# RWKV low-rank products in plain float32, the key norm by tokens, and HGRN projections on the unscaled operand, in a two-layer hybrid decoder on one core

## The chip, the cores and the metric

The kernel runs on one core of one Trainium2 chip. The metric is device time in microseconds (us) of one execution; lower is better. The core has TensorE (PE in the profile; PEld is its weight load), VectorE (DVE), ScalarE (ACT), GpSimd (POOL) and SyncE (SP), which here only issues the weight transfers. Each engine works through its own instruction list in order and waits where a semaphore is not there yet.

## The reference

Two layers, 256 tokens, width 1024, float32. Each layer normalises the hidden state, multiplies it by one wide matrix `w_in`, and feeds column groups to four mixers (RWKV-7, dilated attention, mLSTM, HGRN2). Their outputs are projected, gated, summed and multiplied by `w_out`; a gated feed-forward network follows. What matters here, cut from the reference:

```python
def rwkv7_branch(z, mu, w0, w2, a0, a2, g2, k_k, ...):
    z = z + mu * (token_shift(z) - z)
    r, k, v, wl, al, gl = split_cols(z, [256, 256, 256, 32, 32, 64])
    logw = -softplus(-(w0 + tanh(wl) @ w2)) - 0.5      # low rank 32
    a = sigmoid(a0 + al @ a2)                          # low rank 32
    g = sigmoid(gl) @ g2                               # low rank 64
    kk = heads(k * k_k)                                # 4 heads of 64
    kk = kk * rsqrt(sum(kk * kk, axis=-1, keepdims=True) + 1e-12)
    ...
def hgrn2_branch(z, lower_bound, norm_g):
    q, f, i, g = split_cols(z, [256] * 4)
    ...
# z = rmsnorm(x, gain) @ w_in ; rmsnorm = x * gain * rsqrt(mean(x*x) + eps)
```

The row factor of the norm, `R = rsqrt(mean(x*x) + eps)`, is one number for each token. It may be applied to the operand ahead of the product, or to the product.

## The kernel before, in words

**Precision by splitting.** Weights arrive in blocks of 128 x 1024 (512 KB) in three buffers `raw`. ACT rounds a block to `hi` (line 301) and DVE forms `lo = raw - hi` (line 302). A product takes three reduced-precision (fp32r) matmuls for each 128 x 128 weight tile: hi by hi, hi by lo, lo by hi (lines 351 to 353), 24 for each 128 output columns. SP fetches a block into a `raw` buffer once the `lo` of an earlier block has freed it. Four pairs of `hi` and `lo` may be ahead of TensorE.

**Operand.** `X["u"]` (tiles `xh`, `xl`) is the hidden state times the gain, without the row factor, split in two. `X["s"]` (tiles `sh`, `sl`) is the same with the row factor: `scaled_block` (line 448) forms `xsc` on DVE (line 454) or on ACT and POOL (lines 451, 452), ACT rounds it to `sh` (line 445) and POOL forms `sl` (line 446), for eight blocks. A product on `X["u"]` needs the factor afterwards.

**Row factor.** Two products with a column of ones (`psrm`, line 424) give the sums of squares by token; DVE scales them (`rcm`, line 426); POOL raises them to the power -1/2 (line 427); two products (`psbm`, line 434) spread the result over the partitions, and ACT copies it to `R` (`Rm`, line 437).

**Start of a layer's mixers.** `rw_cols` makes seven RWKV column blocks on `X["u"]` (PSUM tiles `rw`, three PSUM buffers) and evacuates each with `R` into `zr` (lines 610 and 648); between the evacuations it calls `scale`, which makes `X["s"]`. `hg_cols` makes the HGRN columns: `hgq` on `X["u"]` in both layers, `hgf` on `X["u"]` in layer 0 and on `X["s"]` in layer 1, then `hgt` by tokens on `X["s"]`. The gates (`gate`) and everything behind use `X["s"]`.

**RWKV preparation**, a background generator whose pieces are slipped between the large products. It mixes neighbouring tokens (line 659), splits the low-rank weights `lort` into `lw` and the low-rank inputs into `la` (ACT line 670, DVE line 671), stacks the parts on 96 partitions, and multiplies in fp32r (`psw`, `psa`, lines 699 and 700; `psg`, lines 717 and 718). The key norm sums squares by head with a block matrix `bd` (`pss`, line 726), then takes a logarithm and an exponential on ACT (lines 733 and 734), each with a load of ACT's function table.

**Order.** The instruction order of each engine is fixed when the program is built: a scheduler places instructions by its own estimates of when inputs are ready, with the weight splits at a raised priority.

Of the kernel before, what the change touches and what calls it, by code (L numbers as in the profile page):

```python
# [9 lines left out]
F32 = mybir.dt.float32  # L10
# [211 lines left out]
def trunk(tc, x, wst, prm, rows, lora, fing, cfd, cid, out, dbg=None, depth=DEPTH):  # L222
# [160 lines left out]
    def tok_group(name, cols, mid=None):  # L383

        pss = [pmm.tile([128, 512], F32, name=f"{name}{h}", tag="mm") for h in range(2)]
        for kh in range(4):
            hi, lo = w_next()
            for h in range(2):
                for k in range(2):
                    kk = kh * 2 + k  # L390
                    mm3(pss[h][:, :cols], X["s"][0][:, kk, h * 128:(h + 1) * 128], X["s"][1][:, kk, h * 128:(h + 1) * 128],
                        hi[:, k * cols:(k + 1) * cols], lo[:, k * cols:(k + 1) * cols], kk == 0, kk == 7)
# [99 lines left out]
    for l in range(depth):  # L492
        with ExitStack() as lx:
# [12 lines left out]
            with ExitStack() as mxs:  # L506
# [48 lines left out]
                def project(b, kn, m2, quiet=False):  # L555
# [18 lines left out]
                    if m2 == 0:  # L574
                        mop = mp("mop", bufs=1)
                        pad(mop, "padm", 128)
# [26 lines left out]
                R = None  # L603

                def rw_cols():
                    nonlocal R
# [5 lines left out]
                    def scale(ms):  # L612
                        for m in ms:
                            if m % 2 == 0:
                                tmp = gtp.tile([128, 2, T], F32, name="xsc", tag="gt")
                            scaled_block(m, P("gmix", m) if l else pr0[:, m:m + 1], R, tmp[:, m % 2, :])

                    u = X["u"]
                    ps0 = ct_group("rw0", outer=(l > 0), a=u)
                    rc = None  # L620
# [20 lines left out]
                    scale(range(0, 4))  # L641
                    evac(1, ps1)
                    scale(range(4, 8))
# [6 lines left out]
                def rwkv():  # L650
# [18 lines left out]
                    lw = rw.tile([128, 4, 256], F32R, name="lw", tag="bk")  # L669
                    hi_ = lambda d, s_: ac.copy(d, s_)  # L670
                    lo_ = lambda d, s_, h_: ve.tensor_tensor(d, s_, h_.bitcast(F32), op=OP.subtract)
                    for i, r in ((0, 0), (1, 32)):
                        src = lort[r:r + 32, :]
                        hi_(lw[0:32, i], src)
                        hi_(lw[32:64, i], src)
                        lo_(lw[64:96, i], src, lw[r:r + 32, i])
                    hi_(lw[64:128, 2], lort[64:128, :])
                    hi_(lw[0:64, 2], lort[64:128, :])
                    lo_(lw[64:128, 3], lort[64:128, :], lw[64:128, 2])
                    la = rw.tile([128, 3, T], F32R, name="la", tag="ar")  # L680
                    lr = rw.tile([128, T], F32, name="lr", tag="rtmp", bufs=2)
                    ac.activation(lr[0:32, :], zm[0:32, 6, :], AF.Tanh)
                    hi_(la[0:32, 0], lr[0:32, :])
                    hi_(la[64:96, 0], lr[0:32, :])
                    lo_(la[32:64, 0], lr[0:32, :], la[0:32, 0])
                    za_ = zm[32:64, 6, :]
                    hi_(la[32:64, 1], za_)
                    hi_(la[64:96, 1], za_)
                    lo_(la[0:32, 1], za_, la[32:64, 1])
                    ac.activation(lr[64:128, :], zm[64:128, 6, :], AF.Tanh, scale=0.5)  # L690
                    ve.tensor_scalar(lr[64:128, :], lr[64:128, :], 0.5, 0.5, op0=OP.mult, op1=OP.add)
                    hi_(la[64:128, 2], lr[64:128, :])
                    lo_(la[0:64, 2], lr[64:128, :], la[64:128, 2])
# [15 lines left out]
                    sq = rw.tile([128, 2, T], F32, name="rsq", tag="rtmp", bufs=2)  # L709
# [15 lines left out]
                    pss = PS["rw"].tile([128, 2, T], F32, name="pss", tag="rw")  # L725
                    te.matmul(flat(pss), C("bd"), flat(sq), start=True, stop=True)
# [5 lines left out]
                    nk = rw.tile([128, 2, T], F32, name="nk", tag="rtmp", bufs=2)  # L732
                    ac.activation(nk, pss, AF.Ln, bias=eps12)
                    ac.activation(nk, nk, AF.Exp, scale=-0.5)
# [15 lines left out]
                    for n in range(2):  # L750
                        ve.tensor_tensor(bk[0:64, n, :, 1, :], ch(k2)[0:64, n], ch(Wn)[0:64, n], op=OP.mult)
                        ve.tensor_tensor(bk[64:128, n, :, 0, :], ch(k2)[64:128, n], ch(Wn)[64:128, n], op=OP.mult)
                    kk = kkr
                    ve.tensor_tensor(kk, kkr, nk, op=OP.mult)
# [198 lines left out]
                def hg_cols(zz):  # L953
                    for i, nm in enumerate(("q", "f")):
                        direct = l == 0 or i == 0
                        ps = ct_group("hg" + nm, **({"a": X["u"]} if direct else {}))[0][1]
# [598 lines left out]
```

## Time and profile before

| | us |
|---|---|
| median of three runs | 955.33 |
| lowest and highest run | 949.43, 957.17 |
| the profiled execution's own time | 955.37 |
| its span in the trace | 953.5 |

The span is the stretch from the first to the last recorded instruction; the rest of the execution's time, 1.9 us, lies around it. The profile gives each engine's busy time, the idle time ahead of an instruction with what ended it, and the clock that TensorE was granted (1.00 is 2.4 GHz, 0.50 is 1.2 GHz).

### The profile page before, as it was taken

The page shows a single profiled execution, that of the slowest core. Times are in us where ns is not written, and L with a number is a line of the kernel's source. Part 1 is how long each engine was busy: PE and PEld are TensorE (multiplying, and loading weights), DVE is VectorE, ACT ScalarE, POOL GpSimd, SP SyncE. Part 2 cuts the span into 40 slices and gives each one's busy share as a digit, 9 for nine tenths or more (in the row PEclk, how much of TensorE's full clock was granted, in tenths as well). Part 3 has the DMA queues.
Part 4 walks back from the last instruction along what each step waited for, and adds up shares of the span by engine and source line. Part 5 has one row for each costly group of instructions (what it writes and reads, how often), then busy time and mean ns, then how long its engine had stood idle before and what let it go on. Part 6 is the DMA issues. An engine that isn't in the chain of part 4 may idle for free.

```text
span 953.5 us, 22170 instructions
## 1 busy us (share of the span) xinstructions
PE 928.6 (97%) x9072; PEld 880.2 (92%) x9072; DVE 720.6 (76%) x1136; ACT 569.7 (60%) x968; POOL 226.3 (24%) x226
## 2 busy tenths in 40 slices
PE   8899999999999999999999999999999999999996
PEld 6888999999999999999998899999989999999885
DVE  6898566678688998876678975567768889988643
ACT  7784455665466676664478644555745667866533
POOL 2500141111317621110142004211103474211002
PEclk9999999999999999999999999999999999999998
DMA  7544444345475476556555434444536646656561
GB/s 276 177 135 132 126 149 142 134 154 166 144 216 183 146 221 199 187 174 197 189 172 181 147 98 125 154 155 122 188 123 189 201 138 215 230 189 200 182 193 66
DMA packets 48981, 160.12 MB, mean 168 GB/s; under 512 B 5872, under 2 KB 7408, under 8 KB 48752
## 3 DMA queue, kind: packets, MB, share of 16 engines
q1 hardware_dynamic: 46800, 155.03, 50.9%
q10 hardware_dynamic: 1728, 2.62, 0.9%
q8 instruction: 71, 1.16, 0.5%
q0 software_dynamic: 352, 1.06, 0.4%
q14 instruction: 30, 0.25, 0.1%
HBM read 156.06 MB, written 1.05 MB: 165 GB/s over the span
## 4 chain that ended last, share of the span: by engine, by line
PE 74%; DVE 10%; ACT 5%; POOL 4%; issue 4%; DMA 2%; POOLq 0%; SPq 0%; ACTq 0%; DVEq 0%
PE up L353 6%; PE up L351 6%; PE up L352 6%; PE gate L351 6%; PE gate L353 5%; PE gate L352 5%; PE dn L351 4%; PE dn L353 4%; PE dn L352 4%; DVE lo L302 4%; POOL sl L446 2%; POOL xsc L1432 2%; ACT hi L301 2%; DMA raw<-in_wst_dram 1%; PE at L351 1%
## 5 line engine op out<-in xcount | busy, mean ns | idle before, releaser
L302 DVE TENSOR_TENSOR lo<-raw,hi 128x1024 fp32r<-128x1024 f32 (+4 forms) x316 | 377.8, 1201 | 164.7 <-ACT hi L301 155.7
L301 ACT CAST hi<-raw 128x1024 fp32r<-128x1024 f32 (+4 forms) x316 | 307.4, 978 | 275.2 <-PE up L352 47.8
L353 PE MATMUL up<-sh,lo 128*128 128x256 f32 x544 | 152.2, 280 | 0.8 <-DVE lo L302 0.8
L351 PE MATMUL up<-sh,hi 128*128 128x256 f32 x544 | 152.0, 279 | 0.0
L352 PE MATMUL up<-sl,hi 128*128 128x256 f32 x544 | 151.9, 279 | 0.0
L351 PE MATMUL gate<-sh,hi 128*128 128x256 f32 x512 | 146.5, 286 | 0.0
L353 PE MATMUL gate<-sh,lo 128*128 128x256 f32 x512 | 143.0, 279 | 0.0
L352 PE MATMUL gate<-sl,hi 128*128 128x256 f32 x512 | 142.6, 279 | 0.0
L353 PEld LDWEIGHTS up<-sh,lo 128*128 128x128 f32 x544 | 103.4, 190 | 1.4 <-DVE lo L302 1.4
L352 PEld LDWEIGHTS up<-sl,hi 128*128 128x128 f32 x544 | 102.2, 188 | 0.0
L351 PEld LDWEIGHTS up<-sh,hi 128*128 128x128 f32 x544 | 102.2, 188 | 0.0
L351 PEld LDWEIGHTS gate<-sh,hi 128*128 128x128 f32 x512 | 96.5, 188 | 2.3 <-issue 0.2
L353 PEld LDWEIGHTS gate<-sh,lo 128*128 128x128 f32 x512 | 96.2, 188 | 0.6
L352 PEld LDWEIGHTS gate<-sl,hi 128*128 128x128 f32 x512 | 96.3, 188 | 0.4
L1457 POOL TENSOR_TENSOR af<-sf,cvf 128x256 f32<-128x256 f32 x44 | 45.9, 1043 | 157.8 <-ACT sf L1455 157.8
L1453 DVE SCALAR_TENSOR_TENSOR cvf<-up,pr,cvf 128x255 f32<-128x255 f32 (+1 forms) x136 | 65.1, 479 | 2.4
L572 POOL TENSOR_TENSOR merged<-merged,gt 128x512 f32<-128x512 f32 x16 | 26.6, 1666 | 114.3 <-DVE gt L570 114.3
L352 PE MATMUL dn<-alo,hi 128*128 128x256 f32 x176 | 49.5, 281 | 0.0
L353 PE MATMUL dn<-ahi,lo 128*128 128x256 f32 x176 | 49.5, 281 | 0.0
L351 PE MATMUL dn<-ahi,hi 128*128 128x256 f32 x176 | 49.4, 281 | 0.0
L352 PE MATMUL up<-xl,hi 128*128 128x256 f32 x160 | 44.8, 281 | 0.0
L353 PE MATMUL up<-xh,lo 128*128 128x256 f32 x160 | 44.6, 280 | 0.1
(468 smaller groups left out, 2370.0 us busy)
## 6 DMA issues: line engine op xcount, KB each, us to landing
raw<-in_wst_dram SPq DMA_DIRECT2D x254, 512.0 KB, 3.5
raw<-in_wst_dram SPq DMA_DIRECT2D x16, 448.0 KB, 3.2
raw<-in_wst_dram SPq DMA_DIRECT2D x26, 256.0 KB, 2.8
raw<-in_wst_dram SPq DMA_DIRECT2D x8, 392.0 KB, 3.2
zrot<-zrot ACTq DMA_DIRECT2D x24, 64.0 KB, 3.1
cft<-in_cf_dram SPq DMA_DIRECT2D x1, 1041.0 KB, 7.4
hT<-in_x_dram SPq DMA_DIRECT2D x4, 256.0 KB, 6.0
raw<-in_wst_dram SPq DMA_DIRECT2D x8, 128.0 KB, 2.6
```

The source lines that it names most:

```text
L301: ac.copy(hi[:, c], r[:, c])
L302: ve.tensor_tensor(lo[:, c], r[:, c], hi[:, c].bitcast(F32), op=OP.subtract)
L351: te.matmul(o, lh, rh, start=first, stop=False)
L352: te.matmul(o, lh, rl, start=False, stop=False)
L353: te.matmul(o, ll, rh, start=False, stop=last)
L446: gp.tensor_tensor(lo[:, m, :], tmp, h[:, m, :].bitcast(F32), op=OP.subtract)
L572: gp.tensor_tensor(mo, mo, g, op=OP.add)
L1432: gp.tensor_tensor(xsc[:, m, :], xsc[:, m, :], R, op=OP.mult)
L1453: ve.scalar_tensor_tensor(cv[:, n, d:], z[:, n, 0:T - d], P("fcw", 44 * i + cj), cv[:, n, d:], op0=OP.mult, op1=OP.add)
L1457: gp.tensor_tensor(a_, s, cv[:, 0, :], op=OP.mult)
```

## The change

1. `hgf` in layer 1 and `hgt` in both layers use `X["u"]`. The factor is applied at evacuation: to `hgf` by DVE with `R`, to `hgt` by ACT, as its scale operand with one number for each token (`rc`, and half of it, `rch`, a new small DVE instruction).
2. `scale`, which makes `X["s"]`, stands in the program behind the evacuations of `hgq` and `hgf` instead of between those of `rw_cols`.
3. The low-rank products are plain float32 products from the parameters as they lie; the eleven ACT roundings and six DVE subtractions of a layer go.
4. The key norm is by tokens: four small products with an indicator of two heads (`psn`), a DVE addition, a power on POOL (`rn`), and eight products with the identity that spread the result again (`pnk`), which DVE reads from PSUM. The wide product, the logarithm, the exponential and the two table loads go.

```diff
-    def tok_group(name, cols, mid=None):
+    def tok_group(name, cols, mid=None, a=None):
+        ah, al = a or X["s"]
...
                     evac(0, ps0)
-                    scale(range(0, 4))
                     evac(1, ps1)
-                    scale(range(4, 8))
                     evac(2, ps2 or ct_group("rw2", a=u))
...
-                    lw = rw.tile([128, 4, 256], F32R, name="lw", tag="bk")
...
-                        hi_(lw[0:32, i], src)
-                        hi_(lw[32:64, i], src)
-                        lo_(lw[64:96, i], src, lw[r:r + 32, i])
...
-                        te.matmul(psw[:, n, :], lw[0:96, 0, n * 128:(n + 1) * 128], la[0:96, 0], start=True, stop=True)
-                        te.matmul(psa[:, n, :], lw[0:96, 1, n * 128:(n + 1) * 128], la[0:96, 1], start=True, stop=True)
+                        te.matmul(psw[:, n, :], lort[0:32, n * 128:(n + 1) * 128], lr[0:32, :], start=True, stop=True)
+                        te.matmul(psa[:, n, :], lort[32:64, n * 128:(n + 1) * 128], zm[32:64, 6, :], start=True, stop=True)
...
-                        te.matmul(psg[:, h, :], la[:, 2, h * 128:(h + 1) * 128], lw[:, 2], start=True, stop=False)
-                        te.matmul(psg[:, h, :], la[64:128, 2, h * 128:(h + 1) * 128], lw[64:128, 3], start=False, stop=True)
+                        te.matmul(psg[:, h, :], lr[64:128, h * 128:(h + 1) * 128], lort[64:128, :], start=True, stop=True)
...
-                    te.matmul(flat(pss), C("bd"), flat(sq), start=True, stop=True)
+                    psn = PS["rw"].tile([128, 2, 2, 2], F32, name="psn", tag="rw")
+                    for h in range(2):
+                        for n in range(2):
+                            te.matmul(psn[:, h, n, :], sq[:, n, h * 128:(h + 1) * 128], C("ind"), start=True, stop=True)
+                    rn = rw.tile([128, 2, 8], F32, name="rn")
+                    ve.tensor_scalar(rn[:, 0, :], psn.rearrange("p h n q -> p (h n q)"), 1e-12, None, op0=OP.add)
+                    gp.tensor_tensor(rn[:, 1, :], rn[:, 0, :], nhalf, op=OP.pow)
...
-                    ac.activation(nk, pss, AF.Ln, bias=eps12)
-                    ac.activation(nk, nk, AF.Exp, scale=-0.5)
...
+                                te.matmul(pnk[q * 64:q * 64 + 64, n, h * 128:(h + 1) * 128], rn[:, 1, i:i + 1].to_broadcast([128, 64]),
+                                          ident, start=True, stop=True)
-                    ve.tensor_tensor(kk, kkr, nk, op=OP.mult)
+                    ve.tensor_tensor(kk, kkr, pnk, op=OP.mult)
...
-                        if direct:
-                            ve.tensor_tensor(z, ps, bc2(R, 2), op=OP.mult)
-                        else:
-                            ac.copy(z, ps)
+                        ve.tensor_tensor(z, ps, bc2(R, 2), op=OP.mult)
                         zz[nm] = z
-                    pss = tok_group("hgt", 512)
+                        scale(range(i * 4, i * 4 + 4))
+                    pss = tok_group("hgt", 512, a=X["u"])
+                    rch = zp.tile([128, 2], F32, name="rch")
+                    ve.tensor_scalar(rch, rc[:, 0:2], 0.5, None, op0=OP.mult)
...
-                        ac.activation(V[:, h, :], pss[h][:, 0:256], AF.Copy)
-                        ac.activation(tg[:, h, :], pss[h][:, 256:512], AF.Tanh, scale=0.5)
+                        ac.activation(V[:, h, :], pss[h][:, 0:256], AF.Copy, scale=rc[:, h:h + 1])
+                        ac.activation(tg[:, h, :], pss[h][:, 256:512], AF.Tanh, scale=rch[:, h:h + 1])
```

The order that the scheduler makes differs at three places of which the prediction speaks. First TensorE in layer 0, third RWKV column group (`rw_351`; a number behind a name is a buffer). Before, `psbm`, which spreads the row factor, stood 26 products behind `psrm`; here are its nearest neighbours:

```order
L424 MATMUL psrm_345<-ones,acc 128x1 x2
L351 MATMUL rw_351<-xh,hi_232 128x256
L352 MATMUL rw_351<-xl,hi_232 128x256
L353 MATMUL rw_351<-xh,lo_233 128x256
...
L352 MATMUL rw_351<-xl,hi_265 128x256
L434 MATMUL psbm_383<-ident_t,rcm_348 128x128 x2
L353 MATMUL rw_351<-xh,lo_266 128x256
```

Now:

```order
L425 MATMUL psrm_345<-ones,acc 128x1 x2
L351 MATMUL rw_351<-xh,hi_232 128x256
L352 MATMUL rw_351<-xl,hi_232 128x256
L435 MATMUL psbm_383<-ident_t,rcm_348 128x128 x2
L353 MATMUL rw_351<-xh,lo_233 128x256
```

`psbm` moved forward by 24 products and stands two behind `psrm`.

Second, DVE at the same place: the splits `lo`, the row factor `rcm`, and the evacuations `zr`. Before (numbers of the blocks kept):

```order
L302 TENSOR_TENSOR lo4_233<-raw4_193,hi4_232 128x1024
L426 TENSOR_SCALAR rcm0_348<-psrm0_345 128x2
L302 TENSOR_TENSOR lo5_266<-raw5_195,hi5_265 128x1024
L302 TENSOR_TENSOR lo6_318<-raw6_230,hi6_317 128x1024
L302 TENSOR_TENSOR lo7_356<-raw7_263,hi7_355 128x1024
L302 TENSOR_TENSOR lo8_391<-raw8_315,hi8_390 128x1024
L610 TENSOR_TENSOR zr_185<-rw0_187,Rm0_386 128x2x256
```

Now:

```order
L427 TENSOR_SCALAR rcm0_348<-psrm0_345 128x2
L302 TENSOR_TENSOR lo4_233<-raw4_193,hi4_232 128x1024
L949 TENSOR_SCALAR rch_819<-rcm0_348 128x2
L302 TENSOR_TENSOR lo5_266<-raw5_195,hi5_265 128x1024
L617 TENSOR_TENSOR zr_185<-rw0_187,Rm0_386 128x2x256
L617 TENSOR_TENSOR zr_185<-rw1_260,Rm0_386 128x2x256
L455 SCALAR_TENSOR_TENSOR xsc_567<-hT_73,pr0_71,Rm0_386 128x256
...
L455 SCALAR_TENSOR_TENSOR xsc_688<-hT_73,pr0_71,Rm0_386 128x256
L302 TENSOR_TENSOR lo6_318<-raw6_230,hi6_317 128x1024
```

Two evacuations and four `xsc` now stand ahead of the split of block 6; before, the splits of blocks 6 to 8 stood ahead of the first evacuation. `rch` reads the power's result.

Third, ACT at the same place. Before, the copy of the row factor stood behind the roundings of blocks 4 to 8; the last of these and the copy:

```order
L301 CAST hi7_355<-raw7_263 128x1024
L301 CAST hi8_390<-raw8_315 128x1024
L437 COPY Rm0_386<-psbm0_383 128x256
```

Now:

```order
L301 CAST hi5_265<-raw5_195 128x1024
L438 COPY Rm0_386<-psbm0_383 128x256
L301 CAST hi6_317<-raw6_230 128x1024
```

The copy stands ahead of the rounding of block 6. In layer 1 these three places keep their order but for `rch`, which stands one split behind `rcm`. In both layers `psn` stands right ahead of `hgt` and `pnk` 31 products of `hgt` behind it. From about the middle of the gates of HGRN on, TensorE's order is the same in both programs.

## Rows read from the trace of the kernel before

**Rows 1.** The page: busy time and share of each engine.

```profile
PE 928.6 (97%) x9072; PEld 880.2 (92%) x9072; DVE 720.6 (76%) x1136; ACT 569.7 (60%) x968; POOL 226.3 (24%) x226
```

**Rows 2.** TensorE's waits by releaser, 20 to 90 and 480 to 560 us: total, times, longest.

```profile
PE rw L351 <- DVE zr L610: 2.7, 1, 2.7
PE pv L773 <- ACT Vt L781: 0.7, 1, 0.7
PE psrm L424 <- DVE acc L418: 0.6, 1, 0.6
PE psw L699 <- DVE la L671: 0.5, 1, 0.5
...
PE rw L351 <- DVE zr L610: 1.3, 1, 1.3
PE pv L773 <- ACT Vt L781: 1.1, 1, 1.1
```

**Rows 3.** Two windows: length, busy of PE, PEld, DVE, ACT, POOL, granted clock, DMA.

```profile
30.00:40.00 10.00, 7.80 (x54) 7.80 (x55) 9.68 (x12) 8.23 (x20) 9.36 (x10) 0.83 0.40 127
490.00:500.00 10.00, 8.65 (x76) 8.48 (x75) 9.31 (x12) 8.12 (x17) 7.77 (x9) 1.00 0.47 159
```

**Rows 4.** Timeline of PE, layer 0: start, length, instruction, idle time before it.

```profile
22.21 0.61 PE L424 MATMUL psrm<-ones,acc 128*128 128x1 f32 x4 [0.58 <-DVE acc L418]
...
32.20 0.40 PE L351 MATMUL rw<-xh,hi 128*128 128x256 f32 x1 [2.65 <-DVE zr L610]
...
36.66 0.28 PE L351 MATMUL hgq<-xh,hi 128*128 128x256 f32 x1
36.78 0.28 PE L352 MATMUL hgq<-xl,hi 128*128 128x256 f32 x1
```

**Rows 5.** Timelines of ACT and POOL, layer 0.

```profile
27.44 1.05 ACT L301 CAST hi<-raw 128x1024 fp32r<-128x1024 f32 x1 [3.37 <-DMA raw<-in_wst_dram]
30.19 0.37 ACT L437 COPY Rm<-psbm 128x256 f32<-128x256 f32 x1
...
23.59 1.62 POOL L427 TENSOR_TENSOR rcm<-rcm,nhalf 128x2 f32<-128x2 f32 x1 [2.42 <-DVE rcm L426]
```

**Rows 6.** Timeline of DVE, layer 0.

```profile
23.42 2.35 DVE L302 TENSOR_TENSOR lo<-raw,hi 128x1024 fp32r<-128x1024 f32 x2
31.46 0.69 DVE L610 TENSOR_TENSOR zr<-rw,Rm 128x512 f32<-128x512 f32 x1
32.06 1.93 DVE L454 SCALAR_TENSOR_TENSOR xsc<-hT,pr,Rm 128x256 f32<-128x256 f32 x2
```

**Rows 7.** Timeline of ACT, layer 1.

```profile
487.10 2.52 ACT L670 CAST lw<-lort 32x256 fp32r<-32x256 f32 x6 [1.61 <-DMA lort<-in_lora_dram]
...
492.50 0.36 ACT L437 COPY Rm<-psbm 128x256 f32<-128x256 f32 x1
```

**Rows 8.** Timeline of PE, layer 0, low-rank gate product and sums of squares.

```profile
53.84 0.28 PE L717 MATMUL psg<-lw,la 128*128 128x256 f32 x1
54.98 1.13 PE L726 MATMUL pss<-rsq,cft 128*128 128x512 f32 x2
55.54 0.80 PE L352 MATMUL hgt<-lo,sh 128*128 128x512 f32 x1
56.18 0.40 PE L353 MATMUL hgt<-hi,sl 128*128 128x512 f32 x1
```

**Rows 9.** Timelines of PE: plain float32 products elsewhere (a product leaves two records).

```profile
228.40 1.57 PE L1309 MATMUL pS<-cv 64*128 64x256 f32 x12
...
77.01 1.16 PE L792 MATMUL pl<-ar,bk 64*128 64x128 f32 x8
...
89.59 0.95 PE L807 MATMUL psq<-cft,prod 128*128 128x2 f32 x8
```

**Rows 10.** Timelines of ACT (squares of the key, layer 0) and POOL (a power of eight columns).

```profile
48.83 0.63 ACT L712 ACTIVATE rsq<-w4b 128x512 f32<-128x512 f32 x1
...
115.10 1.66 POOL L1131 TENSOR_TENSOR hst<-hst,nhalf 128x8 f32<-128x8 f32 x1 [14.23 <-DMA zrot<-zrot]
```

More of the change, by code (lines that the diff above doesn't have):

```diff
@@ L390, in tok_group @@
                     kk = kh * 2 + k
-                    mm3(pss[h][:, :cols], X["s"][0][:, kk, h * 128:(h + 1) * 128], X["s"][1][:, kk, h * 128:(h + 1) * 128],
+                    mm3(pss[h][:, :cols], ah[:, kk, h * 128:(h + 1) * 128], al[:, kk, h * 128:(h + 1) * 128],
                         hi[:, k * cols:(k + 1) * cols], lo[:, k * cols:(k + 1) * cols], kk == 0, kk == 7)
@@ L575, in project @@
                         mop = mp("mop", bufs=1)
-                        pad(mop, "padm", 128)
+                        pad(mop, "padm", 32)
                         X["m"] = (mop.tile([128, KB, T], F32R, name="mh"), mop.tile([128, KB, T], F32R, name="ml_"))
@@ L601, in trunk, with scale @@
                 gp.memset(zr[:, :, 0:1], 0.0)
-                R = None
+                R = rc = None
+                def scale(ms):
+                    for m in ms:
+                        if m % 2 == 0:
+                            tmp = gtp.tile([128, 2, T], F32, name="xsc", tag="gt")
+                        scaled_block(m, P("gmix", m) if l else pr0[:, m:m + 1], R, tmp[:, m % 2, :])
                 def rw_cols():
-                    nonlocal R
+                    nonlocal R, rc
                     def evac(g, ps):
@@ L610, in evac @@
                             ve.tensor_tensor(zr[:, 2 * g:2 * g + 2, 1:][:, cs_], p_, bc2(R, cs_.stop - cs_.start), op=OP.mult)
[L612 to L616, printed above, removed]
                     u = X["u"]
                     ps0 = ct_group("rw0", outer=(l > 0), a=u)
-                    rc = None
                     def get_rc():
@@ L668, in rwkv @@
                     mix(1, zm[:, 1, :])
-                    lw = rw.tile([128, 4, 256], F32R, name="lw", tag="bk")
[L670 to L673, printed above, removed]
-                        hi_(lw[0:32, i], src)
-                        hi_(lw[32:64, i], src)
-                        lo_(lw[64:96, i], src, lw[r:r + 32, i])
[L677 to L680, printed above, removed]
                     lr = rw.tile([128, T], F32, name="lr", tag="rtmp", bufs=2)
                     ac.activation(lr[0:32, :], zm[0:32, 6, :], AF.Tanh)
[L683 to L689, printed above, removed]
                     ac.activation(lr[64:128, :], zm[64:128, 6, :], AF.Tanh, scale=0.5)
                     ve.tensor_scalar(lr[64:128, :], lr[64:128, :], 0.5, 0.5, op0=OP.mult, op1=OP.add)
-                    hi_(la[64:128, 2], lr[64:128, :])
-                    lo_(la[0:64, 2], lr[64:128, :], la[64:128, 2])
                     rr, kr = zm[:, 0:2, :], zm[:, 2:4, :]
@@ L708, in rwkv @@
                         ac.activation(tha[:, n, :], psa[:, n, :], AF.Tanh, bias=hb_a0[:, n:n + 1], scale=0.5)
-                    sq = rw.tile([128, 2, T], F32, name="rsq", tag="rtmp", bufs=2)
+                    sq = rw.tile([128, 2, T], F32, name="rsq", tag="bk")
                     for n in range(2):
@@ L752, in rwkv @@
                         ve.tensor_tensor(bk[64:128, n, :, 0, :], ch(k2)[64:128, n], ch(Wn)[64:128, n], op=OP.mult)
+                    pnk = PS["rw"].tile([128, 2, T], F32, name="pnk", tag="rw")
+                    for n in range(2):
+                        for h in range(2):
+                            for q in range(2):
+                                i = h * 4 + n * 2 + q
+                                te.matmul(pnk[q * 64:q * 64 + 64, n, h * 128:(h + 1) * 128], rn[:, 1, i:i + 1].to_broadcast([128, 64]),
+                                          ident, start=True, stop=True)
                     kk = kkr
-                    ve.tensor_tensor(kk, kkr, nk, op=OP.mult)
+                    ve.tensor_tensor(kk, kkr, pnk, op=OP.mult)
                     for n in range(2):
```

5 lines of the change are left out of this document (1 added, 4 removed).

## The prediction

> **What bounds the kernel now.** I read the page's busy times first: TensorE is busy 928.6 us of a span of 953.5 [rows 1], so 25 us are all that its idle time could give back, and the edits touch only the start of each layer. Behind the middle of the first gates TensorE's order is the same in both programs; there I expect a plain shift. The second view is the list of TensorE's waits in the two stretches that change: in layer 0 they are 2.7, 0.7, 0.6 and 0.5 us, in layer 1 they are 1.3 and 1.1 [rows 2]. The third is the granted clock: 0.83 in the 10 us from 30 on, so 1.7 us of work lost there, and 1.00 around the shorter wait of layer 1 [rows 3]. So the whole reserve is 4.5 + 1.7 us in layer 0 and 2.4 us in layer 1.
>
> The fourth view, the timelines, shows why TensorE waits. In layer 0 it stops for 2.65 us at block 6, because its three PSUM buffers are full and the first evacuation starts only at 31.46 [rows 4, 6]. That evacuation needs the row factor, whose copy on ACT stands at 30.19 behind roundings that wait for weights from memory, one of them for 3.37 us [rows 5]. The next group, `hgq`, starts at 36.66: block 6 took 4.46 us from 32.20, against 24 x 0.12 = 2.9 us at the pace of `hgq` [rows 4]; the difference is the clock. In layer 1 ACT waits 1.61 us for the low-rank parameters and spends 2.52 us on rounding them, ahead of the weight roundings that the next evacuations queue behind [rows 7].
>
> **The change part by part.**
>
> *The products made plain float32, and the key norm.* Removed on TensorE in each layer: four products of `psw` and `psa`, 4 x 0.12 = 0.5 us [rows 4]; `psg` and `pss` from 53.84 to 55.54, 1.7 us; and the lengthening of the product behind them, 0.80 against 0.40, 0.4 us [rows 8]. That is 2.6 us. Added: `psw` and `psa`, 1,024 columns in all on row groups that start at 0 and 32. The nearest row is `pS`, whose six products (four of 256 columns, two of 128) take 1.57 us [rows 9], 1.23 ns a column, so 1.25 us; the upper bound is the unpaired wide product `pss`, 0.56 + 0.40 us for 512 columns [rows 8], so 1.9 us; I put the lower one at 1.0 by taking off the drain. `psg`, 512 columns without a partner: 0.95 us by `pss`, at least 0.65 by `pS`. `psn`, four products, is the form of `psq`: 0.95 us [rows 9]. `pnk`, eight products of 128 columns: twice the four products of `pl`, 2.3 us [rows 9], or 1.25 by `pS` if its two halves run side by side; nothing says which, so the middle, 1.75. Sum 4.9 us (3.85 to 6.1), net **+2.3 us a layer** (1.25 to 3.5). All of it lies on TensorE's path.
>
> *Off TensorE* the same edit takes away eleven roundings, a logarithm, an exponential and two table loads on ACT, and six subtractions on DVE. I cost their busy time at nothing: behind the starts treated below no wait of TensorE in rows 2 ends with a rounding of weights. If that cover went, they would only help.
>
> *The start of layer 0.* `psrm` waited 0.58 us for the sums of squares [rows 4], which the parameter roundings had delayed on ACT; without them I start it at 21.6. `psbm` now stands two products behind it. The chain between them is the small `rcm` and the power, 1.62 us on POOL [rows 5]; TensorE is at `psbm` at about 22.4 and the power ends at about 24.2: a **new wait of 1.8 us**, with all products of blocks 4 and 5 queued behind it. After `psbm` (0.4) 46 products take 5.5 us: 30.1. On DVE `rch` waits for the same power, and behind it stand the split of block 5 (1.2 us, half of 2.35), two evacuations (0.65 each), four `xsc` (0.96 each) and the split of block 6 [rows 6]: 24.2 + 1.2 + 1.3 + 3.9 + 1.2 = 31.8. TensorE does four products that need no `lo` and waits from 30.6 to 31.8: a **second new wait of 1.2 us**. The old wait is gone, since the first evacuation is done by 26.1. Then 22 products, 2.6 us, end block 6 at 34.4, with two of `hgq` done. Against 36.66 + 0.24 that is **-2.5 us**. It holds that the clock stays up: the new idle times are each shorter than the 2.65 us that was followed by the slow stretch, and 1.35 us in layer 1 was not [rows 2, 3].
>
> Two DVE operands in SBUF are at work here. The `xsc` rows show 0.96 us for 256 columns while POOL makes its own `xsc` and `sl`; an evacuation of 512 columns out of PSUM takes 0.69 [rows 6]. The Trainium skill (SBUF — State Buffer, Who interferes with whom) says that a DVE instruction with two inputs in SBUF contends with a GpSimd one that reads SBUF, and that one with a single SBUF input does not. By that rule the first `xsc`, ahead of POOL's start, would be shorter; at an estimated 0.5 us for all four the second wait would vanish and the sum be 955.0. I keep the row's 0.96, as POOL's work moves along.
>
> *The start of layer 1.* Order and place are kept; the 2.52 us of roundings and the wait of 1.61 for the parameters go from ACT's queue [rows 7], so the splits and evacuations come earlier by more than the 1.35 us that TensorE waited: **-1.3 us**. What is late next is the copy of the row factor, which ended at 492.86 [rows 7], ahead of the wait.
>
> *HGRN on the unscaled operand.* No wait of TensorE on `sh` or `sl` stands in rows 2, so taking `hgf` and `hgt` off them takes no wait away; the scale on ACT replaces an immediate one. The work on `X["s"]` stays as it is and stays early in POOL's and DVE's order; its next reader, the gates, comes some 20 us later. In layer 1 the evacuation of `hgf` moves from ACT to DVE, 0.69 us, off the path. Weight fetches follow the `lo` that free their buffers: block 9's moves from 25.8 to about 31.8, behind the split of block 6; with 3.5 us to landing and two steps it is there at about 38, TensorE at about 40. The waits of `pv` (0.7, 1.1) and `psw` (0.5) I leave as they are.
>
> **Sum.** Layer 0: -2.5 + 2.3 = -0.2. Layer 1: -1.3 + 2.3 = +1.0. Together +0.8 on the profiled execution's 955.37, which is the median of 955.33 to within 0.04: **956.2 us, no difference that can be measured.** Runs of one kernel spread from 949.4 to 957.2, so below about 1% (9.5 us) this kernel cannot be told from no change.
>
> **The rivals.**
>
> *A, the waits go and none takes their place.* All of rows 2 and the slow clock are won, 6.2 + 2.4 us, and the added products cost their lower bound, 2.5: 955.4 - 6.1 = 949.3. For it: every wait in layer 0's start has an input that does come earlier. Against it: `psbm` now stands right behind what it needs.
>
> *B, the small products stand too early on TensorE: slower.* Before, `pss` started 5.5 us after its squares were done (48.83 + 0.63 against 54.98) [rows 8, 10]. `psn` now stands ahead of `hgt`, which TensorE reaches at 34.4 + 5.5 + 5.75 + 1.25 + 0.95 = 47.9; the squares, 2.3 us earlier with `rw` and up to 2.0 with the roundings gone, end between 45.2 and 47.2. A margin of 0.7 to 2.7 us, and ACT's order puts them behind the rounding of a weight block that must have landed. If they are late by 2.7 us in both layers and the clock falls as it did at 30, that is 2 x (2.7 + 1.7) = 8.8 on top of 956.2: 965.0, from where it decides. `pnk` has more cover: 31 products of 0.24 us against a power of 1.66 [rows 10] and two or three DVE steps.
>
> *C, layer 0 gains nothing.* The idle time of 1.8 us pulls the clock down, or block 9 lands late: 956.2 + 2.5 = 958.7.
>
> **How the numbers follow.** Forecast 0.70, A 0.10, B 0.08, C 0.12. The range must leave out at most 2 in 10: 949 takes in A's centre and the lower product costs (-2.1 of the sum); 962 takes in C with the upper costs (+2.4) and the milder part of B, one layer's wait. Faster by over 1% is half of A, 0.05; slower is B, 0.08; the rest, 0.87, lies within 1%.
>
> **What would show it.** Right: a wait at `psbm` of about 1.8 us ended by POOL and one of about 1.2 at block 6 ended by `lo`; a clock of 1.00 from 30 to 40; `hgq` begun near 31 and done near 40; no wait of `rw` in layer 1; 4 to 6 us in a layer for `psw`, `psa`, `psg`, `psn` and `pnk` together; the same distance between `gate` and the end as before. Wrong: a slow clock anywhere behind 20 us, a wait at `psn` or `pnk` ended by ACT or POOL, or a changed length of the stretch from the gates on.

## The result, and the profile after

The changed kernel takes **949.0 us** (median of 12 runs, 947.1 to 954.8) against 954.1 for the kernel before beside it: ratio 0.9946, interval 0.9925 to 0.9967. On a second chip it was 948.3 against 953.4, again 0.9946 (0.9924 to 0.9967). It is about 5 us faster. The forecast of 956.2 was wrong in sign; 949.0 lies on the edge of its range. The profiled execution shown here took 949.1 us, its span is 947.3. Medians and ratios in this document leave out the few executions that took over 1.5% more than the fastest of their kernel.

Busy time and share of each engine, to set beside [rows 1]:

```profile
PE 927.8 (98%) x9124; PEld 879.2 (93%) x9124; DVE 715.3 (76%) x1129; ACT 554.5 (59%) x937; POOL 230.0 (24%) x228
```

TensorE's waits of the changed kernel from 20 to 90 us (for 480 to 560 the list is empty), beside [rows 2]:

```profile
PE psbm L435 <- POOL rcm L428: 1.6, 1, 1.6
PE pv L760 <- ACT Vt L768: 1.2, 1, 1.2
PE rw L353 <- DVE lo L302: 0.9, 1, 0.9
PE psg L694 <- ACT w4a L683: 0.6, 1, 0.6
```

The first and third are the two new waits that the prediction names; the wait of `rw` in layer 1 is gone. The windows beside [rows 3] (length, busy of PE, PEld, DVE, ACT, POOL, granted clock, DMA) show full clock from 30 to 40, and a later stretch that is not full:

```profile
30.00:40.00 10.00, 9.14 (x80) 8.93 (x78) 10.00 (x11) 7.02 (x14) 9.56 (x8) 1.00 0.61 185
240.00:250.00 10.00, 9.16 (x65) 9.16 (x65) 4.55 (x7) 3.53 (x5) 1.58 (x1) 0.83 0.31 103
```

TensorE's timeline at the start of layer 0, beside [rows 4]; the first `hgq` product starts at 30.03, the last at 39.00:

```profile
21.55 0.50 PE L425 MATMUL psrm<-ones,acc 128*128 128x1 f32 x4
24.02 0.71 PE L435 MATMUL psbm<-ident_t,rcm 128*128 128x128 f32 x4 [1.63 <-POOL rcm L428]
30.03 0.28 PE L351 MATMUL hgq<-xh,hi 128*128 128x256 f32 x1
...
31.28 0.39 PE L353 MATMUL rw<-xh,lo 128*128 128x256 f32 x1 [0.86 <-DVE lo L302]
```

The added products on TensorE's timeline, layer 0, beside [rows 8, 9]:

```profile
40.12 0.48 PE L676 MATMUL psw<-lr,lort 32*128 32x256 f32 x1
40.12 0.48 PE L677 MATMUL psa<-zr,lort 32*128 32x256 f32 x1
...
45.27 1.13 PE L694 MATMUL psg<-lort,lr 64*128 64x256 f32 x4 [0.62 <-ACT w4a L683]
...
47.81 0.95 PE L705 MATMUL psn<-cft,rsq 128*128 128x2 f32 x8
...
55.90 1.09 PE L738 MATMUL pnk<-ident_t,rn 128*64 128x128 f32 x16
```

**Where the time came from.** I cut both kernels' timelines at the same products and took each piece in all profiles there are, four of before and three of the changed kernel (the later ones are among the experiments). Medians in us:

| stretch, cut at the start of a product | forecast | before | changed | difference |
|---|---|---|---|---|
| layer 0: start to last `hgq` | -2.5 | 41.1 | 38.6 | -2.6 |
| to last `hgt` | +2.3 | 20.1 | 22.1 | +2.0 |
| to last product of the first gates | 0 | 38.5 | 36.9 | **-1.6** |
| layer 1: first `rw` to last `hgq` | -1.3 | 27.2 | 26.0 | -1.2 |
| to last `hgt` | +2.3 | 19.4 | 21.5 | +2.1 |
| to last product of the first gates | 0 | 39.2 | 35.8 | **-3.4** |
| sum | +0.8 | | | -4.7 |

Four of the six terms came out within 0.3 us. The two that the forecast put at zero hold the whole miss of these stretches.

That the sum is so near the measured 5 us is partly luck. Behind the first gates, where the forecast has a plain shift, the changed kernel is slower. From the last product of the first gates to the last product of all gates stand 1,927 records in the same order in both kernels. With half clock taken off, this stretch takes 168.1 us before and 169.1 now in layer 0, 168.4 and 169.2 in layer 1 (medians of the same profiles): +1.8 us. One profile of each for layer 1, before and then changed, with PE alone:

```profile
567.33:735.67 168.34, 166.43 (x1929) 1.00 0.47 148
559.86:729.07 169.21, 167.30 (x1929) 1.00 0.47 146
```

The granted clock goes the other way; the table holds only a part of it (see the section on the clock).

**The first gates.** Between the gate products stand small ones: the RWKV scores `pl` and the HGRN products `pdl`. Two lines each, of before and then of the changed kernel: the windows of the first gates of layer 0 for `pl` alone and for `pdl` alone (columns as above; the `pl` lines have no ACT and POOL, the `pdl` lines no POOL).

```profile
62.04:100.61 38.57, 4.62 (x32) 3.86 (x32) 2.56 (x4) 1.00 0.42 129
62.04:100.61 38.57, 5.78 (x192) 4.56 (x192) 3.56 (x12) 0.00 (x0) 1.00 0.42 129
```

```profile
61.10:97.93 36.83, 3.47 (x32) 2.90 (x32) 2.65 (x4) 1.00 0.40 131
61.10:97.93 36.83, 4.02 (x192) 3.35 (x192) 3.40 (x12) 0.00 (x0) 1.00 0.40 131
```

As many records, 2.9 us less of busy time: 1.15 on `pl`, 1.76 on `pdl`. In layer 1 the four sums are the same (4.62, 5.78, 3.47, 4.02). Busy time runs to modelled ends; from start to next start it is 2.5 us, 1.08 on `pl` and 1.41 on `pdl`, in both layers. `pdg`, now in two visits instead of one, and `pv` give 0.4 of it back. The wait for `pv` went from 0.7 to 1.2 in layer 0 and from 1.1 to none in layer 1, which is why layer 1 gained more. That accounts for both stretches to within 0.3 us. TensorE's timeline shows what changed in `pl` and `pdl`; the kernel before:

```profile
77.01 1.16 PE L792 MATMUL pl<-ar,bk 64*128 64x128 f32 x8
78.10 0.30 PE L1074 MATMUL pdl<-qsb,kt 64*64 64x32 f32 x4
78.33 1.16 PE L792 MATMUL pl<-ar,bk 64*128 64x128 f32 x8
79.42 0.30 PE L1074 MATMUL pdl<-qsb,kt 64*64 64x32 f32 x4
...
81.13 1.15 PE L792 MATMUL pl<-ar,bk 64*128 64x128 f32 x8
82.21 0.30 PE L1074 MATMUL pdl<-qsb,thq 64*64 64x32 f32 x4
82.45 1.16 PE L792 MATMUL pl<-ar,bk 64*128 64x128 f32 x8
```

and the changed one:

```profile
68.60 1.16 PE L779 MATMUL pl<-ar,bk 64*128 64x128 f32 x8
...
70.35 1.16 PE L779 MATMUL pl<-ar,bk 64*128 64x128 f32 x8
...
76.21 1.16 PE L779 MATMUL pl<-ar,bk 64*128 64x128 f32 x16
77.30 0.67 PE L1060 MATMUL pdl<-qsb,kt 64*64 64x32 f32 x32
```

A product leaves two records, so x8 is four products. Before, the scores come as four visits of four products of one row group (rows 0 to 63 or 64 to 127), 1.09 us each from start to next start, and break the rows of `pdl` into pieces. Now the last eight come in one visit, alternating between the row groups, and eight take the same 1.09 us. `pdl` comes in six visits instead of eleven.

### The profile page after: what moved, and what is told of

Read it like the earlier page. It is cut to its first block, busy times and chain, and to the rows that moved or that the text cites. A ratio compares the mean times of both kernels' runs of the same rounds, so it can differ in the third digit from the quotient of the medians.

```text
span 947.3 us, 22239 instructions
## 1 busy us (share of the span) xinstructions
PE 927.8 (98%) x9124; PEld 879.2 (93%) x9124; DVE 715.3 (76%) x1129; ACT 554.5 (59%) x937; POOL 230.0 (24%) x228
## 3 DMA queue, kind: packets, MB, share of 16 engines
q0 software_dynamic: 352, 1.06, 0.4%
## 4 chain that ended last, share of the span: by engine, by line
PE 85%; DVE 7%; POOL 4%; issue 2%; DMA 1%; ACT 1%; POOLq 0%; SPq 0%; ACTq 0%; DVEq 0%
PE up L353 7%; PE up L351 7%; PE gate L351 7%; PE up L352 7%; PE gate L353 6%; PE gate L352 6%; PE dn L351 4%; PE dn L352 4%; PE dn L353 4%; DVE lo L302 2%; POOL sl L447 2%; POOL xsc L1418 2%; PE wo L352 2%; PE wo L351 2%; PE wo L353 2%
```

## The experiments

Medians of the runs; "before" is the kernel before on the same chip. The variants ran on several chips, on which the kernel before has 953.4 to 955.4. The ratio is as recorded, up to 0.002 away from the quotient of the two medians.

| kernel | median | before | ratio and interval |
|---|---|---|---|
| changed, again | 948.3 | 953.4 | 0.9946 (0.9924 to 0.9967) |
| low-rank edit alone | 951.3 | 954.1 | 0.9972 (0.9942 to 1.0003) |
| key norm alone | 956.0 | 954.1 | 1.0018 (0.9991 to 1.0045) |
| HGRN and scaled operand alone | 958.6 | 954.1 | 1.0051 (1.0021 to 1.0081) |
| changed without the low-rank edit | 957.4 | 953.4 | 1.0023 (0.9995 to 1.0052) |
| changed, both rows of scores joined | 948.8 | 954.1 | 0.9955 (0.9929 to 0.9981) |
| changed, scores by row group | 951.3 | 954.4 | 0.9973 (0.9941 to 1.0004) |
| before, second row joined | 961.1 | 955.4 | 1.0069 (1.0040 to 1.0098) |
| changed, wait filled | 950.2 | 954.4 | 0.9970 (0.9938 to 1.0003) |
| old key norm, rows joined | 947.7 | 953.4 | 0.9935 (0.9910 to 0.9960) |
| low-rank edit, rows joined | 944.8 | 953.4 | 0.9908 (0.9875 to 0.9941) |
| the same, wait filled | 942.9 | 954.4 | 0.9901 (0.9861 to 0.9941) |

### One edit at a time

The low-rank edit on the kernel before:

```diff
-    te.matmul(psw[:, n, :], lw[0:96, 0, n * 128:(n + 1) * 128], la[0:96, 0], ...)
+    te.matmul(psw[:, n, :], lort[0:32, n * 128:(n + 1) * 128], lr[0:32, :], ...)
```

> The kernel before with the plain float32 low-rank products alone; key norm, HGRN and the scaled operand as before. My theory: this edit alone makes the order of the changed kernel (psbm two products behind psrm, the scores pl of the second pair of heads in one unbroken row), so it has the whole gain and pays less for products: start of layer 0 -3.0 us, start of layer 1 -1.4, first gates -2 to -3.4 in each layer, products +0.5 a layer instead of +2: about 8 us under before, 946, and 3 under the changed kernel. Rival 1 (every edit has a share of the gain, by the work that it takes off ScalarE): about 952. Rival 2 (the measured gain is the luck of the two paces of the wide products, not the edit): 949 to 957, with no row of the trace ahead of 100 us showing it.

The order came as expected, the time half-way: 951.3, interval up to 1.0003, so not told from no change. Its timeline has the joined row of scores (`pl` x16 at 77.41) and the first gates take 35.1 and 35.4 us in the two layers, even less than in the changed kernel. What took it back in the profiled run is a wait ahead of `psw`, with half clock behind it from 43 to 49.5. TensorE's waits from 20 to 110:

```profile
PE psw L678 <- ACT lr L670: 1.9, 1, 1.9
PE psbm L434 <- POOL rcm L427: 1.6, 1, 1.6
PE rw L353 <- DVE lo L302: 0.9, 1, 0.9
```

The key norm by tokens on the kernel before (edit 4 of the change alone):

> The kernel before with the key norm by tokens alone. My theory: psbm and the scores stay where they were or worse (all four groups of pl apart), the norm's small products cost about 1 us a layer more than the wide one they replace, the start waits stay: 955 to 957. Rival 1 (shares): about 952, by the logarithm, the exponential and two table loads taken off ScalarE. Rival 2: anywhere from 949 to 957.

956.0, as expected: no gain by itself.

The HGRN edits and the place of `scale` on the kernel before (edits 1 and 2 alone, with the padding of a buffer cut from 128 to 32 bytes, which is in the change's program too):

> The kernel before with the edits on HGRN and on the place of the scaled operand alone. My theory: psbm stays 26 products behind psrm, TensorE's wait of 2.65 us at block 6 and the slow clock behind it stay, the scores stay apart: 954, no difference. Rival 1 (shares): about 952, since HGRN no longer waits for the scaled operand. Rival 2: anywhere from 949 to 957.

958.6: slower by 4.5 us, where I expected nothing. By the mean granted clock of the runs, 0.9882 against 0.9912, some 2.8 us of it are lost clock. The profile has no single step for it; TensorE waits 1.7 us at `psw`, 1.6 at `rw` in layer 1 and 0.7 at `pl`, and there are four stretches of half clock.

The changed kernel with the split low-rank products back:

> The changed kernel with the split low-rank products back; key norm by tokens and the HGRN edits stay. My theory (the low-rank edit alone moves psbm forward and lets the scores run in one row): the start of layer 0 as before, all four groups of pl apart, all added products of the key norm paid: 957 (955 to 960), slower than before. Rival (the other two edits bring half of the gain): 951.

957.4, as expected, though it can't be told from the kernel before. Its scores stand in four visits again, and the start waits are those of before in another mix (20 to 110 us):

```profile
PE psw L697 <- DVE la L669: 1.7, 1, 1.7
PE psrm L425 <- DVE acc L419: 1.4, 1, 1.4
PE rw L351 <- DVE zr L617: 0.7, 1, 0.7
```

The low-rank edit carries the gain: of these four kernels and the two compared, those with it have `psbm` two products behind `psrm` and the joined scores, those without it have neither, and without it the rest of the change is no faster than before. The effects don't add: -2.8, +1.9 and +4.5 alone, -5.1 together. The rival of equal shares falls.

### The grouping of the scores

One idle step of the generator moved from behind the first scores to ahead of them:

```diff
+                        for _ in range(1 * (n == 0)):
+                            yield
                         pls = [PS["rw"].tile(...) for _ in range(2)]
...
-                        yield
-                        yield
+                        for _ in range((1, 2)[n]):
+                            yield
```

> The changed kernel with one idle step of the RWKV generator moved from behind the first scores to ahead of them, so that the scores pl of the first pair of heads, too, run as eight products in a row that alternate between row groups 0 and 64, as those of the second pair do. Nothing else of TensorE's order changes behind the middle of the first gates. My theory (four products of one row group take 1.08 us, eight that alternate 1.09; each break between large products costs some 0.2): -1.1 -0.2 in each layer, 946.4 against the changed kernel's 949.0. Rival (the grouping costs nothing, the gates' gain came from the missing wait for Vt alone): 949.

The trace did as expected: both visits are x16, and the first gates take 35.4 and 34.2 us, 1.5 less than in the changed kernel in each layer. Of that 1.08 are on the scores and 0.4 on the gate products around them, which are broken off at two places fewer.

```profile
71.61 1.16 PE L780 MATMUL pl<-ar,bk 64*128 64x128 f32 x16
...
76.24 1.16 PE L780 MATMUL pl<-ar,bk 64*128 64x128 f32 x16
```

The median did not: 948.8. The mean granted clock of its runs is 0.9933 against 0.9947 and 0.9957 of the changed kernel; (1 - clock) x 950 us makes that 6.3 us of lost clock against 5.1 and 4.1, so by this estimate one to two of the three microseconds went there. Why is open.

The changed kernel with its last scores issued row group by row group:

```diff
-                        for j in range(4):
-                            for par in range(2):
+                        for par in range(2):
+                            for j in range(4):
```

> The changed kernel with the scores pl of the second pair of heads issued row group by row group (four products on rows 0 to 63, then four on rows 64 to 127), where the changed kernel alternates; their place is the same. If products of one row group follow each other at 0.27 us and those that alternate run side by side, the second block of scores takes 2.2 us instead of 1.1 in each layer: +2.2 us, 951. Rival (the block's cost is its entry and exit, not its products): no change, 949.

951.3. The visit starts at 75.34 and the next work at 76.98, 1.64 us where alternating takes 1.09:

```profile
75.34 1.71 PE L779 MATMUL pl<-ar,bk 64*128 64x128 f32 x16
76.98 0.67 PE L1060 MATMUL pdl<-qsb,kt 64*64 64x32 f32 x32
```

In the first 0.55 us of the visit four records start; in the changed kernel, which alternates, eight (`pl` alone, PE alone):

```profile
75.33:75.88 0.55, 0.54 (x4) 1.00 1.00 320
```

```profile
76.20:76.75 0.55, 0.54 (x8) 1.00 0.96 290
```

So the truth lies between the two readings. By the starts of the single records, those of one row group follow each other every 0.112 us, which makes 0.90 us for four products. The first and the last record of a visit take some 0.1 us more each: together the 1.09 us. When the row groups alternate, two records start 0.007 us apart and the next two 0.112 us after them, so eight products take no longer than four. Row group after row group would be 1.98 us at that pace; it is 1.64, because some records of the second group still start beside those of the first. The Trainium skill (TensorE: Matmul & The Clock Gate, Why this matters for your kernels) says that products on distinct row groups run at the same time; the 1.09 us for eight agree.

The kernel before, all its arithmetic kept, with two idle steps ahead of the first scores:

```diff
+                        for _ in range(2 * (n == 0)):
+                            yield
                         pls = [PS["rw"].tile(...) for _ in range(2)]
```

> The kernel before, all arithmetic unchanged, with two idle steps of the RWKV generator ahead of the first scores, so that the scores of the second pair of heads run as eight products that alternate between the row groups, and fewer of the small HGRN products stand between them; what follows in the generator comes two steps later. If the grouping alone is worth the time of the first gates: from the end of hgt to the last gate product of that branch 1.6 us less than in before in each layer, 951 in all. Rival (without the low-rank edit the later steps only shift the cost on to the products behind): 954 or more.

Both sides of the expectation came true. The first gates take 35.8 and 35.9 us, 2.8 and 3.3 less than before. Of that 1.4 us are no gain: `px` and `pd`, 64 records each that stand in this stretch in the kernel before, start only behind it. The 1.5 and 1.9 us that are left are 1.08 on the scores, 0.24 on `pdl` and a shorter wait at `pv` (0.4 for 0.7, 0.7 for 1.1): the grouping is worth its time without the low-rank edit. But the generator ends two steps later, the mLSTM work behind it slips, and TensorE waits where it did not before (200 to 300 us), followed by half clock: 961.1.

```profile
PE pyC L588 <- DVE y_ml L1330: 3.1, 2, 2.7
PE pp L351 <- ACT yhC L592: 0.7, 1, 0.7
```

### The clock, and repeats

> The changed kernel once more, on one chip with the three below. In the runs so far the mean granted clock was 0.9947 for it and 0.9912 for the kernel before; a stretch at half clock of 3.4 us costs 1.7 us and lowers the mean by 0.0018, so about 3 of the 5 us between them would be such stretches, which follow waits of TensorE of over a microsecond, and 2 would be the work itself. If so: 949 again, clock 0.994 to 0.995, and before again at 0.991. Rival (two chips were compared): no difference of the clocks on one chip, and less than 3 us between the kernels.

The repeat holds: 948.3; mean clock 0.9957 against 0.9918 over 26 runs of before, which is 7.8 - 4.1 = 3.7 us of lost clock. The means of these runs, 948.6 and 953.8, differ by 5.2 us, so 1.5 are left for the work. The profiles agree: the table's -4.7 without the 1.3 us of clock that is in it (below), and the +1.8 behind the first gates, make -1.6. (The group `up` is left out, whose pace differs from one profile to the next; see the last section.) To see whether TensorE's idle time makes it, six products that nobody reads fill the wait at `psbm`:

```diff
+            fil = PS["mx"].tile([128, 512], F32, name="fil", tag="mx")
+            for _ in range(6):
+                te.matmul(fil, u[0][:, 0, 0:128], ...)
             R = row_bcast(f"m{l}", rc)
```

> The changed kernel with six products of 512 columns (operands that lie there already, the result is never read) ahead of the two products between psrm and psbm, so that TensorE works through most of its 1.6 us wait for the row factor; the rest of its order is the same. If idle time of that length is what the granted clock falls after (in one profile of the changed kernel it fell right behind this wait, in another it did not), the mean clock over the runs rises by about 0.001 to 0.002 from 0.995 and the time falls by 1 to 1.7 us, to 947; no profile shows half clock between 20 and 30 us. Rival (the falls come whether or not TensorE waits there): clock and time as in the changed kernel, 948.5 to 949, or 0.2 more since the fillers end late.

The wait is down to 0.2 us, the time is not: 950.2, mean clock 0.9945, one stretch of half clock all the same, at 217 us (0.50, 1.2 GHz).

```profile
PE pv L764 <- ACT Vt L772: 1.4, 1, 1.4
PE rw L353 <- DVE lo L302: 0.9, 1, 0.9
PE psbm L435 <- POOL rcm L428: 0.2, 1, 0.2
```

So my reading that this wait costs the clock found no support. Four single profiles, to see where the clock falls:

> The kernel before once more, for a second profile of it. By the mean granted clock over the runs (0.9918 against 0.9957) it should show more than one stretch of half clock behind the first 20 us, each behind a wait of TensorE of over a microsecond (psrm, block 6 of rw, psw), where the first profile shows one; the stretch from the end of hgt to the middle of the first gates should again be 1.6 us longer than in the changed kernel in layer 0 and 3.4 in layer 1.

> A third profile of the kernel before. If the clock is lost at the starts of the layers: a stretch of half clock of 3 to 6 us between 20 and 60 us, behind the wait at block 6, psrm or psw. Rival (anywhere): none there, one or two elsewhere.

> A fourth profile of the kernel before, with the same two readings: a stretch of half clock between 20 and 60 us, or only elsewhere. With four profiles, two or more with such a stretch against none or one of five of the changed order would bear the first out.

> A third profile of the changed kernel: no half clock between 30 and 60 us; from hgt's end to the middle of the first gates 30.6 us in layer 0 and 35.7 in layer 1, as in its first two; a stretch of half clock at most at 20 to 30 us (wait for the row factor) or at 205 to 250.

The lengths of the first gates repeat in all of them, within 0.2 us in layer 0 and 0.6 in layer 1. The clock: behind the wait at block 6 (2.2 to 2.65 us) three of the four profiles of before show half clock between 32 and 37 us; the second, with 2.6 us of wait, does not, and has one stretch behind the first 20 us where I expected more. (All seven profiles have half clock in their last 3 to 6 us, too, and four of them have it ahead of 14 us.) None of three profiles of the changed kernel has any there. The window from 30 to 40 us, third profile of before, then third of the changed kernel:

```profile
30.00:40.00 10.00, 8.39 (x58) 8.39 (x59) 10.00 (x12) 8.22 (x18) 9.96 (x10) 0.83 0.43 142
```

```profile
30.00:40.00 10.00, 9.52 (x82) 9.35 (x84) 10.00 (x11) 6.44 (x12) 8.76 (x7) 1.00 0.63 206
```

Such a stretch costs 1.7 us, so this place gives up to 1.3 us on the mean and is in the -2.6 of the table. It gives less where a later wait takes it back: in the second profile of before TensorE waits 1.7 us at `psw`, against 0.2 to 0.5 in the others, and it is at the last `hgt` at 61.5 us, against 62.0, 61.6 and 60.8. Elsewhere two of the four profiles of before have one (705 to 713 us) and two of the three of the changed kernel (217 to 245). The one left, the second of the changed kernel, has it at 24 to 28, behind the wait of 1.6 us at `psbm`. The rest of the clock's 3.7 us, seen over many runs, has no place in these profiles and stays open.

### Versions that beat both

The changed kernel with the old key norm and both rows joined:

> The changed kernel with the old key norm (one wide product, logarithm, exponential) and the scores of both pairs of heads in one row each. My theory: psn and pnk (0.8 + 1.0 us a layer) go, pss (1.0) comes back, the row of scores is as in the kernel with pairs alone: about 1 to 2 us under that one, 947. Rival (the key norm by tokens is what makes the key early enough): a wait at the scores or at pv of over 1 us in each layer, 951.

The kernel before with the low-rank edit and both rows joined:

> The kernel before with the plain float32 low-rank products and the scores of both pairs of heads in one row each; everything else as before. My theory: the kernel with the low-rank edit alone (951.3) less 1.5 us a layer: 948. Rival (the place of the scaled operand has to move too, since ScalarE is late at psw without it): a wait at psw of about 2 us and half the clock behind it, as in the kernel with the low-rank edit alone, and 950 or more.

The same with the six filling products:

> The fastest kernel so far (low-rank edit and rows of scores, 944.8) with the same six products in TensorE's wait for the row factor. If the clock theory holds, one stretch of half clock fewer in some of the runs: 943.5. Rival: no change, 945.

947.7, 944.8 and 942.9: the last two are the fastest, and the fill can't be told from none. In the profile of the first the wait that its rival names came in layer 0 alone: 2.3 us at `pv`, with half clock behind it from 66 to 70. In layer 1 of the second, the stretch to the last `hgt` is 20.7 us (21.5 in the changed kernel, the tokens' norm costs 0.75 us a layer more than the wide product), the first gates 34.2. What I feared in it came and cost less than I thought: 1.6 us at `psw`, with the clock full from 30 to 60.

```profile
PE psw L678 <- ACT lr L670: 1.6, 1, 1.6
```

## Why the prediction was wrong, point by point

- **The start of layer 0 was right**, mechanism and size: -2.6 for -2.5. The new wait at `psbm` is 1.63 for 1.8, that at block 6 is 0.86 for 1.2, the clock stays up from 30 to 40. Some of the size is luck. `psrm` starts 1.1 us earlier by the medians, where the sum has 0.6, and it starts 0.4 to 1.0 us later where there is half clock at 9 to 13 us, as in three of four profiles of before and one of three of the changed kernel. On DVE two errors cancel in part. The first `xsc` took 0.47 us, as POOL was idle when it started, and the next three 0.95 to 0.97 with POOL at work: 3.0 us for 3.9. The split behind them took 1.76 us, also with POOL at work, for 1.2. The rule of the Trainium skill (SBUF — State Buffer, Who interferes with whom) is that a VectorE instruction with two inputs in SBUF contends with a GpSimd one that reads SBUF; the trace agrees with it in both. The prediction's estimate of 0.5 us held for one `xsc` of four.

```profile
26.42 0.47 DVE L455 SCALAR_TENSOR_TENSOR xsc<-hT,pr,Rm 128x256 f32<-128x256 f32 x1
26.81 2.73 DVE L455 SCALAR_TENSOR_TENSOR xsc<-hT,pr,Rm 128x256 f32<-128x256 f32 x3
```

- **The start of layer 1 was right**: -1.2 for -1.3, the wait gone in all profiles with the low-rank edit. It was missing in one of four profiles of before, so it is not owed in every run.
- **The products were nearly right**: +2.0 and +2.1 for +2.3. `psw` and `psa` 1.06, `psg` 1.06, `psn` 0.81, `pnk` 1.03 from start to next start: 4.0 us for 4.9. The mis-sized term is `pnk`, 1.03 for 1.75: its halves do run side by side. The row of `pS` was misread: its six products are three of 256 and three of 128 columns, 1.36 ns a column, which would make `psw` and `psa` 1.4 us. The net came out near only because less went away, too: 1.9 us for 2.6. In layer 1 the products of `hgf` between the small ones take 0.46 us more than before, and the lengthening behind `pss` was 0.17, not 0.4. In layer 0 `psg` brought a wait of 0.6 on ACT that no part of mine had.
- **The step that failed is the sum itself**, "Layer 0: -2.5 + 2.3 = -0.2. Layer 1: -1.3 + 2.3 = +1.0." It has no term between the end of `hgt` and the middle of the first gates. I had the plain shift begin behind that middle, left `pv` as it was, and priced nothing in between, though TensorE's order changes there. That stretch gave -1.6 and -3.4. With it the same sum is +0.8 - 5.0 = -4.2, or 951.2. Two more things stand at nothing in it: the plain shift, where the gates took 1.8 us more, and the clock outside block 6, 2.4 us less lost over many runs. With both it is -4.8; what sets these two stays open.
- **"Off TensorE ... I cost their busy time at nothing" was the wrong question.** Their busy time is off the path; but the scheduler places small products when it estimates their inputs to be ready, and eleven roundings fewer moved that estimate, hence the order. Where the scheduler's estimate moved is inferred from the orders; that the low-rank edit is what moves them is shown.
- **The rivals.** A gave 949.3, a hit by accident: the waits that it says don't come came. B did not come: `psn` starts 3.8 us behind its squares (43.97), `pnk` waits for nothing. C did not come as a whole, but in one profile of three half clock did follow its idle time (24 to 28 us). That cost some 0.5 us up to the last `hgq` (18.0 us from `psrm`, against 17.5 and 17.6), since the wait at block 6 fell away.
- **Of its signs of being wrong two came**: a slow clock behind 20 us, in each profile of the changed kernel (at 24, 217 and 242 us), and a changed length from the gates on.

## What to carry to other kernels

- In a kernel whose order a scheduler makes, take every stretch where the two orders differ and price it, also where the same instructions stand in it: here 2.5 us a layer came from the same 224 records in another grouping. Then measure the stretches where the orders agree, too: a plain shift was off by 1.8 us.
- Small float32 products pay for each visit between large products (for the scores here some 0.2 us of their own and 0.2 on the gate products around them) and run two for one when they alternate between row groups. Count visits and row groups before counting columns.
- Work taken off an engine that bounds nothing can still move the engine that does. And one profile is one draw: cut the time into stretches and take each over several profiles before believing a difference of a few microseconds.

## What I had not expected of the hardware

**Two paces at one granted clock.** The same products of the same order (`up`, layer 0, 350 to 400 us, fully busy, clock 1.00), kernel before, then changed:

```profile
350.00:400.00 50.00, 50.00 (x427) 50.00 (x426) 18.03 (x38) 10.08 (x18) 1.00 0.63 198
```

```profile
350.00:400.00 50.00, 50.00 (x444) 50.00 (x443) 18.19 (x38) 10.91 (x20) 1.00 0.65 206
```

427 products against 444, 117 ns against 113 each, 4%. A third profile of before has 443 there, one of a changed variant 427: in this group it belongs to no kernel. From the last gate to layer 1's first product, at full clock, it makes 213.1, 212.4, 207.9 and 213.1 us in the four profiles of before, against 207.4 to 208.3 in the three of the changed kernel. So the difference of two single profiles drifts by up to 5 us where their orders agree. The runs fall apart in the same way: with the lost clock taken off, 22 of the 26 runs of before on the second chip lie at 943 to 947 us and four at 950.5 to 952, which is part of their spread of 949.9 to 960.2.

In the gates a slower pace goes with the kernel. The third gates of layer 1 take 54.19 us in all four profiles of before and with the low-rank edit alone, but 54.64 in all three of the changed kernel and in the changed one without the low-rank edit. What sets the pace was not found.
